# Reordering the middle stage of a two-layer hybrid encoder step: sample keys, prompt pairs, sample output, GLU

## The chip, the core and the metric

The kernel runs on one core of one Trainium2 chip. Its time is the device time of one execution in microseconds. Five engines matter here. PE (TensorE) does matrix products and transposes, with PEld loading its weights. DVE (VectorE), ACT (ScalarE) and POOL (GpSimd) do elementwise work. SP does nothing here but issue DMA transfers from its queue. Each engine works through its own list of instructions strictly in that list's order.

## The reference

The model has two layers over a prompt of 2048 tokens and a sample of 64 tokens with a cache of 2048 latents. Only the first layer is touched. In it one projection feeds two branches, latent attention and a state-space layer (S5) with a GLU:

```python
q   = (rms_norm(q_lat, g_q_lat) @ w_uq).reshape(B, T, 8, 96)        # 64 plain + 32 rotary
q_n, q_r = rms_norm(q[..., :64], ...), rope(rms_norm(q[..., 64:], ...), pos)
k_n = rms_norm(einsum('bkc,chd->bkhd', lat_all, w_uk), g_k_nope)   # lat_all = cache + new for the sample
v   = einsum('bkc,chd->bkhd', lat_all, w_uv)
o_mla = attend_chunk_causal(...)   # prompt        o_mla = attend(...)   # sample
z = gelu(s5_scan(u, ...))
z = z * sigmoid(z @ w_glu + b_glu)                                 # 512 x 512 product per token
mixed = concat([o_mla * silu(gate_mla), z * silu(gate_s5)])
return x + mixed @ w_out, ...
```

For the sample, attention multiplies the probabilities with the latents first and with w_uv afterwards.

## The kernel before

The program has four phases: a (projections, up to 540 us), b (the middle stage, up to about 921 us), c (prompt attention, up to about 1455 us) and d (output projection and the convolution layer). Products are made as three products of split numbers (`mm3`, lines L71 to L73: high by high, low by high, high by low); ACT makes the high half and DVE or POOL the low half by a subtraction. A scheduler in the compiler orders each engine's list from the order in which the program is written and from a model of durations; the buffers of a pool can be reused only when all readers of the previous pool are done.

Phase b, `phase_b`, runs so. `stage1` computes the scores of the sample queries against 17 chunks of keys (`km`, `ka`, `kb`, `sc`; the scores stay in `sT`, their running maximum in `smax`) and beside them the 16 pairs of the S5 output (`pa`, `pb`: `s5_pair`, `o_w`, `o_u`, result `s_z`). Then two generators run in turns: `phase_glu` (four column groups q of 528 tokens; for each, four loads of z and four of the gate g, a split into `g_zh` (ACT) and `g_zl` (POOL), 96 products into `pp`, a tanh, two DVE operations, and a split of the result into `g_mh` (ACT) and, in place of z, by POOL (L1224)) and `sample_av`. `sample_av` takes the maximum over keys into `mrow`, subtracts it (DVE L1115), exponentiates (ACT L1116), adds up the 17 chunks on POOL into `psum` (L1117), multiplies with the latents `lat` on PE (L1124, two accumulators), forms the reciprocal of the sum with a few small PE steps, and multiplies with w_uv (L1154). Then the weights w_uq, w_uk, w_uv are loaded and split again, and eight pairs of prompt blocks follow (`p_load`, `p_mm`, `p_norm`, `p_tr`): a pair loads `i_ql` and `i_cT`, makes queries (`pq`), keys and values (`pp`), stores the values (L664), normalizes, transposes and stores `s_kT` and `s_qT`. The rest of the GLU runs between their steps. After phase b, the buffers of the head with index 0 (`c_kx`) are opened, and phase c loads head 0 in four pieces and splits them on ACT and DVE (L1279, L1280); heads from 1 on are split on POOL (L1282, L1283), which also scales every softmax row (L1319).

## Time and profile before

| what | value |
| --- | --- |
| runs | 2441.78, 2442.80, 2450.74 us, median 2442.8 us |
| profiled execution | 2443.96 us, span 2442.1 us |
| busy share of the span | PE 92%, PEld 82%, DVE 76%, ACT 48%, POOL 58% |
| granted PE clock, mean | 0.969 of full speed |
| chain that ended last | PE 63%, DVE 8%, DMA 6%, ACT 3%, POOL 2% |
| bytes moved | 354 MB, 145 GB/s mean |

The profiled execution is about 1 us above the median of the runs; all sums below are made against its own time of 2443.96 us. PE is busy nearly all the time except in the middle stage: of 40 equal slices of the span the page gives PE 7, 6 and 8 tenths in those around 690, 750 and 930 us. The chain's shares say which engine the end waited for; a busy share in itself does not, since an idle engine off that chain costs nothing.

### The profile page before, as it was taken

What the parts mean: (1) busy time and instruction counts of PE and PEld (TensorE: products, weight loads), DVE (VectorE), ACT (ScalarE), POOL (GpSimd) and SP (SyncE); (2) the same over time, 40 slices, a digit from 0 to 9 for tenths busy, and PEclk for the clock granted to TensorE, in tenths of its full rate; (3) what the DMA queues carried; (4) which work ended last, traced back from release to release, by engine and by line L of the source; (5) the groups of instructions that cost most, each with busy time, mean ns of one, the idle gap of its engine ahead of it and who ended that gap; (6) DMA issues with size and microseconds to landing.
All of it is one profiled execution on the core that took longest, in us unless ns stands there. A gap on an engine that the chain in (4) does not pass through costs nothing.

```text
span 2442.1 us, 39230 instructions
## 1 busy us (share of the span) xinstructions
PE 2245.7 (92%) x13613; PEld 2004.2 (82%) x13613; DVE 1861.3 (76%) x3986; ACT 1181.5 (48%) x2196; POOL 1413.3 (58%) x1281
## 2 busy tenths in 40 slices
PE   6788989989986987999999999999999999989996
PEld 6788979986655876888888888988888889879996
DVE  7772346975473776888787865999999999999994
ACT  4343345236543665777777754433433533533433
POOL 5232543117382545777777444586768888876861
PEclk9999999999998997999999999999999999999998
DMA  8887575326665873222222337665355346434452
GB/s 190 198 221 166 132 177 151 87 63 186 162 161 155 257 221 85 72 69 67 69 70 70 92 126 255 235 186 177 103 172 180 95 129 212 146 127 134 147 171 89
DMA packets 347590, 354.29 MB, mean 145 GB/s; under 512 B 149760, under 2 KB 285248, under 8 KB 347392
## 3 DMA queue, kind: packets, MB, share of 16 engines
q1 hardware_dynamic: 346688, 350.60, 50.5%
q8 instruction: 108, 1.77, 0.3%
q10 hardware_dynamic: 704, 1.18, 0.2%
q14 instruction: 90, 0.74, 0.1%
HBM read 257.91 MB, written 93.52 MB: 144 GB/s over the span
## 4 chain that ended last, share of the span: by engine, by line
PE 63%; DVE 8%; DMA 6%; ACT 3%; issue 2%; POOL 2%; SPq 1%; DVEq 0%; ACTq 0%; POOLq 0%
PE pp L71 14%; PE pp L72 14%; PE pp L73 14%; PE pt L1338 4%; PE s_ps L1295 3%; PE o L1359 2%; PE o L1358 2%; PE s_ps L1296 2%; PE s_ps L1297 2%; DMA kl<-s_kT 1%; DMA s_v<-v_hl 1%; DVE acc L1648 1%; DVE sT L1115 1%; PE ps L552 1%; PE ps L550 1%
## 5 line engine op out<-in xcount | busy, mean ns | idle before, releaser
L1648 DVE SCALAR_TENSOR_TENSOR acc<-vt,cw,acc 128x384 f32<-128x384 f32 (+2 forms) x1142 | 671.2, 660 | 2.1 <-ACT acc L1634 0.5
L1844 POOL TENSOR_TENSOR wl<-wr,wh 128x1024 fp32r<-128x1024 f32 x110 | 265.3, 2413 | 119.6 <-ACT wh L1843 119.6
L1843 ACT ACTIVATE wh<-wr 128x1024 fp32r<-128x1024 f32 x136 | 144.1, 1060 | 325.7 <-PE pp L72 166.8
L1348 DVE TENSOR_TENSOR ptl<-pt,pth 128x512 fp32r<-128x512 f32 (+2 forms) x320 | 186.2, 602 | 30.2 <-ACT pth L1347 29.0
L1347 ACT ACTIVATE pth<-pt 128x512 fp32r<-128x512 f32 (+2 forms) x320 | 161.9, 528 | 92.4 <-PE pt L1338 90.6
L71 PE MATMUL pp<-b0h,wh 128*128 128x512 f32 (+1 forms) x488 | 181.3, 372 | 7.6 <-ACT b0h L1751 6.0
L73 PE MATMUL pp<-b0h,wl 128*128 128x512 f32 (+1 forms) x488 | 180.4, 370 | 0.0
L72 PE MATMUL pp<-b0l,wh 128*128 128x512 f32 (+1 forms) x488 | 180.3, 370 | 0.0
L1319 POOL TENSOR_SCALAR s_sb<-s_sb,s_st 128x1024 f32<-128x1024 f32 (+7 forms) x128 | 118.3, 937 | 103.7 <-DVE s_st L1315 65.4
L1844 POOL TENSOR_TENSOR w<-wr,w 128x1024 fp32r<-128x1024 f32 x57 | 137.4, 2410 | 61.6 <-ACT w L1843 59.2
L71 PE MATMUL pp<-xh,vh 128*128 128x256 f32 (+1 forms) x448 | 133.3, 298 | 31.8 <-ACT vh L191 12.0
L1843 ACT ACTIVATE w<-wr 128x1024 fp32r<-128x1024 f32 x64 | 67.9, 1060 | 175.2 <-PE pp L72 103.4
L1359 PE MATMUL o<-ptl,v 128*128 128x256 f32 x576 | 150.7, 299 | 0.1
L1358 PE MATMUL o<-pth,v 128*128 128x256 f32 x576 | 149.0, 285 | 0.7 <-ACT pth L1347 0.6
L1295 PE MATMUL s_ps<-kh,qh 96*128 96x512 f32 (+3 forms) x320 | 132.7, 415 | 11.4 <-DVE s_sm L1300 9.9
L73 PE MATMUL pp<-xh,vl 128*128 128x256 f32 (+1 forms) x448 | 131.5, 294 | 1.7 <-DVE mx L208 1.7
L71 PE MATMUL pp<-xh,wh 128*128 128x256 f32 (+1 forms) x384 | 115.0, 299 | 19.0 <-ACT qsum L229 10.9
L72 PE MATMUL pp<-xl,vh 128*128 128x256 f32 (+1 forms) x448 | 131.8, 294 | 0.0
L1338 PE MATMUL pt<-ident,s_sb 128*128 128x128 f32 x800 | 121.4, 277 | 11.2 <-POOL s_sb L1319 8.6
L1311 ACT ACTIVATE s_sb<-s_sb,s_st 128x1024 f32<-128x1024 f32 (+6 forms) x128 | 122.0, 956 | 8.7 <-DVE s_st L1303 8.3
L1296 PE MATMUL s_ps<-kh,ql 96*128 96x512 f32 (+3 forms) x320 | 117.1, 366 | 0.0
L1297 PE MATMUL s_ps<-kl,qh 96*128 96x512 f32 (+3 forms) x320 | 117.0, 366 | 0.0
(521 smaller groups left out, 7606.8 us busy)
## 6 DMA issues: line engine op xcount, KB each, us to landing
wr<-w_c SPq DMA_DIRECT2D x120, 512.0 KB, 3.5
wr<-w_o SPq DMA_DIRECT2D x80, 512.0 KB, 3.6
raw<-xT SPq DMA_DIRECT2D x28, 512.0 KB, 5.0
raw<-x SPq DMA_DIRECT2D x16, 512.0 KB, 5.5
s_v<-v_hl SPq DMA_DIRECT2D x8, 1024.0 KB, 7.2
tb<-s_x SPq DMA_DIRECT2D x32, 256.0 KB, 3.1
raw<-w_m SPq DMA_DIRECT2D x15, 512.0 KB, 6.9
v<-s_v SPq DMA_DIRECT2D x15, 512.0 KB, 5.1
```

What stands on the lines that cost most here:

```text
L71: mm(o, wh, xh, start=first, stop=False)
L72: mm(o, wh, xl, start=False, stop=False)
L73: return mm(o, wl, xh, start=False, stop=last)
L1295: nc.tensor.matmul(o[:, :n], t["qh"][:, q], t["kh"][:, k0:k0 + n], start=True, stop=False)
L1296: nc.tensor.matmul(o[:, :n], t["ql"][:, q], t["kh"][:, k0:k0 + n], start=False, stop=False)
L1338: nc.tensor.transpose(p[:, i, :], sb[:, (c + i) * 128:(c + i + 1) * 128], self.ident)
L1348: nc.vector.tensor_tensor(ptl[:, c:c + m, e:e + 128], p[:, :m, :], f(pth[:, c:c + m, e:e + 128]), op=OP.subtract)
L1358: nc.tensor.matmul(w, v[:, c, :], pth[:, c, lo:], start=c == 0, stop=False)
L1359: nc.tensor.matmul(w, v[:, c, :], ptl[:, c, lo:], start=False, stop=c == 2 * a + 1)
L1648: stt(box[i], vt[:, k:k + n], cw[:, ct, k:k + 1], src, op0=OP.mult, op1=OP.add)
L1843: act(h, r, AF.Copy)
L1844: (nc.vector if vec_split(slots[i]) else nc.gpsimd).tensor_tensor(l, r, f(h), op=OP.subtract)
```

## The change

Phase b is written in another order. After `stage1` the maximum is taken at once (`av_max`), then the pairs run alone, with the split w_uq and w_uk that phase a left in place (`self.bw`) instead of reloaded ones. Then the buffers of head 0 are opened, and `sample_av` and `phase_glu` follow, so the GLU runs last and alone. The sum of the exponentials is a third product per chunk, with ones as weights, into a third accumulator; POOL's additions, the zeroing of `psum` and the small products for the sum go away, and the reciprocal is taken on 128x512 numbers in place of 128x4. The latents are loaded in four pieces of 512 KB, the GLU weights in one of 1 MB, ahead of the pairs. In `stage1` two S5 pairs stand ahead of the first cache loads, and the rotary table of the sample shrinks to the rows that it needs.

```diff
@@ -137,9 +137,10 @@
...
-            x = cp.tile([128, G, 32], F32, name=tr + nm)
-            nc.sync.dma_start(x, A[tr])
-            nc.gpsimd.tensor_tensor(x, x, g[:, None, :].to_broadcast([128, G, 32]), op=OP.mult)
+            n = rows.stop - rows.start
+            x = cp.tile([128, n, 32], F32, name=tr + nm)
+            nc.sync.dma_start(x, A[tr][:, rows])
+            nc.gpsimd.tensor_tensor(x, x, g[:, None, :].to_broadcast([128, n, 32]), op=OP.mult)
@@ -427,8 +428,8 @@
...
+            pp = self.pool(es, "b_pp", 3, PSUM)
...
-            pp = self.pool(es, "b_pp", 3, PSUM)
@@ -449,9 +450,9 @@
...
-            def q_mm(sp, qp, w, m, pq, pn):
+            def q_mm(sp, qp, w, m, pq, pn, bufs=2):
...
-                raw = sp.tile([128, 2, 384], F32, name="q_raw")[:m]
+                raw = sp.tile([128, 2, 384], F32, name="q_raw", bufs=bufs)[:m]
@@ -495,7 +496,7 @@
             def stage1():
...
-                self.rope_tab(s1, "q", math.sqrt(32.0))
+                self.rope_tab(s1, "q", math.sqrt(32.0), slice(16, 17))
@@ -560,15 +561,17 @@
...
-                raw, sq = q_mm(s1, (q[:, 0], q[:, 1]), wuq, 64, pp, "pp")
+                raw, sq = q_mm(s1, (q[:, 0], q[:, 1]), wuq, 64, pp, "pp", 1)
...
+                pa(0)
+                pa(1)
...
-                pa(0)
-                q = q_norm(s1, raw, st, 16, 64)
+                pb(0)
+                q = q_norm(s1, raw, st, 0, 64, 1)
@@ -585,8 +588,8 @@
...
-                PIPE = ((lc_load, 4), (km, 3), (ka, 2), (kb, 1), (sc, 0), (pa, 1), (pb, 0))
-                seen = {lc_load: 4, km: 1, pa: 1}
+                PIPE = ((lc_load, 4), (km, 3), (ka, 2), (kb, 1), (sc, 0), (pa, 2), (pb, 1))
+                seen = {lc_load: 4, km: 1, pa: 2, pb: 1}
@@ -605,29 +608,15 @@
...
-            self.s5es.close()
-            eg = ExitStack()
-            glu = self.phase_glu(eg, pp)
-            att = self.sample_av(eav, ap, pt)
-            NA = 10
-            for i in range(16):
-                next(glu, None)
-                if i < NA:
-                    for _ in range(18 * (i + 1) // NA - 18 * i // NA):
-                        next(att, None)
-                if i == NA:
-                    for _ in att:
-                        pass
-                    eav.close()
-                    break
+            hs = self.pool(eav, "h_s", 1)
+            self.av_max(ap, pt)
+            wgr = hs.tile([128, 4, 512], F32, name="wg_r")
+            nc.sync.dma_start(wgr, A["w_glu"])
...
+                sp = self.pool(e2, "b_s", 2)
...
-                sp = self.pool(e2, "b_s", 2)
...
-                wuq = load_w(sp, wp, "w_uq", 3, 768)
-                wuk = load_w(sp, wp, "w_uk", 2, 512)
-                wuv = load_w(sp, wp, "w_uv", 2, 512)
-                self.rope_tab(wp, "q", math.sqrt(32.0))
+                wuq, wuk = self.bw["w_uq"], self.bw["w_uk"]
@@ -698,23 +687,39 @@
...
+                wuv = load_w(sp, wp, "w_uv", 2, 512)
+                self.rope_tab(wp, "q", math.sqrt(32.0))
...
-                        next(glu, None)
...
-                        next(glu, None)
...
-                for _ in glu:
-                    pass
-                eg.close()
+            self.s5es.close()
+            self.kxes = ExitStack()
+            self.kx = self.pool(self.kxes, "c_kx", 1, None, "right")
+            eg = ExitStack()
+            eacc = ExitStack()
+            glu = self.phase_glu(eg, pp, wgr)
+            att = self.sample_av(eacc, hs, pt)
+            for i in range(16):
+                for _ in range(2):
+                    next(att, None)
+                next(glu, None)
+                if i == 8:
+                    for _ in att:
+                        pass
+                    eacc.close()
+                    eav.close()
+            for _ in glu:
+                pass
+            eg.close()
@@ -1054,7 +1059,7 @@
...
-        w = sp.tile([128, 2, 2, 128], F32, name="o_w", bufs=2)
+        w = sp.tile([128, 2, 2, 128], F32, name="o_w", bufs=3)
@@ -1074,76 +1079,69 @@
...
-    def sample_av(self, es, cp, pt):
+    def av_max(self, sp, pt):
+        nc = self.nc
+        p = pt.tile([128, 512], F32, name="pt").rearrange("p (a b) -> p a b", a=4)
+        for i in range(4):
+            nc.tensor.transpose(p[:, i], self.smax[:, i * 128:i * 128 + 128], self.ident)
+        st = sp.tile([128, 4], F32, name="st")
+        nc.vector.tensor_reduce(st, p, axis=AX.X, op=OP.max)
+        self.mrow = sp.tile([128, 512], F32, name="mrow")
+        o = pt.tile([128, 512], F32, name="pt")
+        for i in range(4):
+            self.bcast(o[:, i * 128:i * 128 + 128], st[:, i:i + 1], 128)
+        nc.scalar.copy(self.mrow, o)
+
+    def sample_av(self, es, sp, pt):
...
-        sp = self.pool(es, "h_s", 2)
...
-
-        def rows(col):
-            o = pt.tile([128, 512], F32, name="pt")
-            for i in range(4):
-                self.bcast(o[:, i * 128:i * 128 + 128], col[:, i:i + 1], 128)
-            return o
-
-        p = pt.tile([128, 512], F32, name="pt").rearrange("p (a b) -> p a b", a=4)
-        for i in range(4):
-            nc.tensor.transpose(p[:, i], self.smax[:, i * 128:i * 128 + 128], self.ident)
-        st = sp.tile([128, 8], F32, name="st", bufs=1)
-        nc.vector.tensor_reduce(st[:, :4], p, axis=AX.X, op=OP.max)
-        mrow = sp.tile([128, 512], F32, name="mrow", bufs=1)
-        nc.scalar.copy(mrow, rows(st))
-        acc = [pl.tile([128, 512], F32, name=f"acc{i}") for i in range(2)]
-        psum = sp.tile([128, 512], F32, name="psum", bufs=1)
-        nc.vector.memset(psum, 0.0)
+        acc = [pl.tile([128, 512], F32, name=f"acc{i}") for i in range(3)]
...
-        XB = 3
-
-        def load(i):
-            c = order[i]
-            if c < 16:
-                lat[c] = sp.tile([128, 256], F32, name="lat", bufs=XB)
-                nc.sync.dma_start(lat[c], A["latc"][128 * c:128 * c + 128])
+        wv = sp.tile([128, 2, 512], F32, name="wv")
+        gm = sp.tile([128, 4, 64], F32, name="o_g")
+
+        def load(b):
+            t = sp.tile([128, 4, 256], F32, name="lat", bufs=2)
+            nc.sync.dma_start(t, A["latc"][512 * b:512 * b + 512].rearrange("(c p) d -> p c d", p=128))
+            for i in range(4):
+                lat[4 * b + i] = t[:, i]
...
-            tt(x, x, mrow[:m], op=OP.subtract)
+            tt(x, x, self.mrow[:m], op=OP.subtract)
...
-            nc.gpsimd.tensor_tensor(psum[:m], psum[:m], x, op=OP.add)
...
         def av(i):
...
-            x = self.sT[:64 if c == 16 else 128, c]
+            m = 64 if c == 16 else 128
+            x = self.sT[:m, c]
+            mm(acc[2], self.ones[:m].to_broadcast([m, 128]), x, start=i == 0, stop=i == 16)
+            l = self.clat_s if c == 16 else lat.pop(c)
...
-                l = self.clat_s[:, k * 128:k * 128 + 128] if c == 16 else lat[c][:, k * 128:k * 128 + 128]
-                mm(acc[k], l, x, start=i == 0, stop=i == 16)
-            lat.pop(c, None)
-
-        for i in range(XB):
-            load(i)
-        for i in range(4):
+                mm(acc[k], l[:, k * 128:k * 128 + 128], x, start=i == 0, stop=i == 16)
+
+        load(0)
+        load(1)
+        for i in range(3):
...
+        nc.sync.dma_start(wv, A["w_uv"])
+        nc.sync.dma_start(gm, S["gm"][:, :, TP:].rearrange("h p t -> p h t"))
         for i in range(17):
...
-            if i + XB < 17:
-                load(i + XB)
-            if i + 4 < 17:
-                prob(i + 4)
+            if i and i % 4 == 0 and i // 4 + 1 < 4:
+                load(i // 4 + 1)
+            if i + 3 < 17:
+                prob(i + 3)
...
-        wv = sp.tile([128, 2, 512], F32, name="wv", bufs=1)
-        nc.sync.dma_start(wv, A["w_uv"])
-        p = pt.tile([128, 512], F32, name="pt")
-        for i in range(4):
-            mm(p[:, i:i + 1], psum[:, i * 128:i * 128 + 128], self.ones, start=True, stop=True)
-        nc.vector.reciprocal(st[:, 4:8], p[:, :4])
-        r = sp.tile([128, 512], F32, name="rrow", bufs=1)
-        act(r, rows(st[:, 4:8]), AF.Copy)
-        pls = sp.tile([128, 2, 512], F32, name="pls", bufs=1)
+        r = sp.tile([128, 512], F32, name="rrow")
+        nc.vector.reciprocal(r, acc[2])
+        pls = sp.tile([128, 2, 512], F32, name="pls")
@@ -1152,18 +1150,16 @@
...
-            g = sp.tile([128, 64], F32, name="o_g")
-            nc.sync.dma_start(g, S["gm"][hp, :, TP:])
-            r_ = sp.tile([128, 64], F32, name="o_r")
-            tt(r_, o, g, op=OP.mult)
-            rh = sp.tile([128, 64], F32R, name="o_h")
-            rl = sp.tile([128, 64], F32R, name="o_l")
+            r_ = sp.tile([128, 64], F32, name="o_r", bufs=2)
+            tt(r_, o, gm[:, hp], op=OP.mult)
+            rh = sp.tile([128, 64], F32R, name="o_h", bufs=2)
+            rl = sp.tile([128, 64], F32R, name="o_l", bufs=2)
...
-    def phase_glu(self, es, pg):
+    def phase_glu(self, es, pg, wr):
@@ -1177,10 +1173,8 @@
...
-            r = cp.tile([128, 512], F32, name="wg_r", bufs=2)
-            nc.sync.dma_start(r, A["w_glu"][:, k])
-            act(wh[:, k], r, AF.Copy)
-            gt(wl[:, k], r, f(wh[:, k]), op=OP.subtract)
+            act(wh[:, k], wr[:, k], AF.Copy)
+            gt(wl[:, k], wr[:, k], f(wh[:, k]), op=OP.subtract)
@@ -1232,8 +1226,8 @@
...
+            sp = self.pool(es, "c_s", 2)
...
-            sp = self.pool(es, "c_s", 2)
@@ -1921,8 +1915,6 @@
...
-            k.kxes = ExitStack()
-            k.kx = k.pool(k.kxes, "c_kx", 1, None, "right")
```

The list of DVE after the last score of `stage1` (smax). `g_g` and `g_r` belong to the GLU, `sT`/`mrow` to the sample softmax, `w_uvl` to the weights of the pairs, `st<-k_sq`, `st<-q_sq` and `v_hl` to the first pair. Before:

```order
L1211 TENSOR_TENSOR g_g<-g_z,g_g 128x528
L1221 SCALAR_TENSOR_TENSOR g_g<-g_r,g_g 128x264
L1095 TENSOR_REDUCE st<-pt 128x4
L1221 SCALAR_TENSOR_TENSOR g_g<-g_r,g_g 128x264
L1115 TENSOR_TENSOR sT<-sT,mrow 64x512
L1115 TENSOR_TENSOR sT<-sT,mrow 128x512 x16
L1241 MEMSET mq 1x64
L1244 MEMSET mk 1x64
L1221 SCALAR_TENSOR_TENSOR g_g<-g_r,g_g 128x264 x3
```

With the change (lines have moved by two and more, so L1115 is L1117 now):

```order
L555 TENSOR_TENSOR smax<-ps,smax 128x512 x8
L1088 TENSOR_REDUCE st<-pt 128x4
L1117 TENSOR_TENSOR sT<-sT,mrow 64x512
L1117 TENSOR_TENSOR sT<-sT,mrow 128x512 x16
L605 TENSOR_TENSOR w_uvl<-q_raw,w_uvh 128x512 x2
L645 TENSOR_REDUCE st<-k_sq 128x8 x2
L466 TENSOR_REDUCE st<-q_sq 128x8
L467 TENSOR_REDUCE st<-q_sq 128x8
L650 TENSOR_TENSOR v_hl<-pp,v_hl 128x4x64 x2
```

All 17 subtractions, and the maximum before them, now stand ahead of the first reductions and splits of the pairs, with no GLU operation between.

The list of SP around the first loads of the GLU (`g_z`, `g_g`; `bg` and `wg_r` are its bias and weights, `s_z` the stores of the S5 output, `kr_r` rotary keys of the cache, `o_h`/`o_l` the sample output, `s_qT`/`s_kT` the last pair's results, `kl` keys of head 0). Before:

```order
L1177 DMA bg<-b_glu 128x4
L1181 DMA wg_r<-w_glu 128x512 x2
L1058 DMA o_w<-s_w_72 128x512
L1075 DMA s_z<-o_z 128x2x266
L510 DMA kr_r<-krcT 32x256
L1181 DMA wg_r<-w_glu 128x512 x2
L1075 DMA s_z<-o_z 128x2x266 x2
L1191 DMA g_z<-s_z 128x8x66
L1195 DMA g_g<-s_gs 128x8x66
```

With the change:

```order
L685 DMA s_kT<-k_t 64x4x256 x2
L1261 DMA kl<-s_kT 64x512
L686 DMA s_qT<-q_t 96x8x256
L1159 DMA s_mx_h<-o_h 128x64
L1160 DMA s_mx_l<-o_l 128x64
L1159 DMA s_mx_h<-o_h 128x64
L1185 DMA g_z<-s_z 128x8x66
L1189 DMA g_g<-s_gs 128x8x66
```

The GLU's first z load stood behind stores of the S5 output; it stands now behind two stores of `o_h` and one of `o_l`.

The list of POOL at the end of phase b (`q_t`, `q_n`: last pair; `g_z<-g_g,g_mh` and `g_zl`: GLU; `kh`, `qh`, `kl`: head 1; `s_sm`: softmax rows of head 0). Before:

```order
L481 TENSOR_TENSOR q_t_9728<-q_xr,cosTq 128x256
L482 TENSOR_TENSOR q_t_9729<-q_xr,sinTq 128x256
L483 TENSOR_TENSOR q_n<-q_t_9728,q_t_9729 128x8x16
L484 TENSOR_TENSOR q_n<-q_t_9728,q_t_9729 128x8x16
L1282 TENSOR_SCALAR kh<-kl 96x512 x2
L1319 TENSOR_SCALAR s_sm<-s_sm,s_st 128x128
L1283 TENSOR_TENSOR kl<-kl,kh 96x512
L1282 TENSOR_SCALAR qh<-ql 96x512 x2
L1283 TENSOR_TENSOR kl<-kl,kh 96x512
L1319 TENSOR_SCALAR s_sm<-s_sm,s_st 128x256
L1319 TENSOR_SCALAR s_sm<-s_sm,s_st 128x384
```

With the change:

```order
L1218 TENSOR_TENSOR g_z<-g_g,g_mh 128x8x66 x5
L1204 TENSOR_TENSOR g_zl<-g_z,g_zh 128x528 x4
L1218 TENSOR_TENSOR g_z<-g_g,g_mh 128x8x66 x4
L1204 TENSOR_TENSOR g_zl<-g_z,g_zh 128x528 x4
L1218 TENSOR_TENSOR g_z<-g_g,g_mh 128x8x66 x4
L1313 TENSOR_SCALAR s_sm<-s_sm,s_st 128x128
L1276 TENSOR_SCALAR kh<-kl 96x512 x2
L1313 TENSOR_SCALAR s_sm<-s_sm,s_st 128x256
L1313 TENSOR_SCALAR s_sm<-s_sm,s_st 128x384
L1277 TENSOR_TENSOR kl<-kl,kh 96x512
```

Before, the last pair's rotary work stood ahead of the first heads; now the last two column groups of the GLU do. Of head 1 the two splits of `kh` stand ahead of the second softmax row in both.

## Rows read from the trace of the kernel before

**Rows 1.** Windows: stretch, length, busy us of PE, PEld, DVE, ACT, POOL, PEclk, DMA share, GB/s
```profile
750.00:770.00 20.00, 7.62 (x30) 6.55 (x30) 3.39 (x4) 3.05 (x4) 3.56 (x3) 0.68 0.80 250
...
920.00:940.00 20.00, 8.81 (x25) 5.70 (x25) 4.99 (x20) 5.64 (x15) 10.80 (x14) 0.50 0.95 225
```

**Rows 2.** Chain that ended last, 640 to 780 us: start, us, what
```profile
674.79 17.04 DVE sT L1115 x10
```

**Rows 3.** Timeline of PE, stage1: start, us, what, idle before and its releaser
```profile
550.81 0.80 PE L71 MATMUL pp<-bw,lc_h 128*128 128x512 f32 x1 [5.68 <-ACT lc_h L517]
...
651.61 1.12 PE L550 MATMUL ps<-qrb,kr_r 32*128 32x512 f32 x2 [0.32 <-DVE smax L554]
...
655.24 1.12 PE L550 MATMUL ps<-qrb,kr_r 32*128 32x512 f32 x2 [0.32 <-DVE smax L554]
...
666.43 1.12 PE L550 MATMUL ps<-qrb,kr_r 32*128 32x512 f32 x2
...
668.40 0.37 PE L71 MATMUL pp<-g_zh,wgh 128*128 128x264 f32 x1
```

**Rows 4.** Sample softmax by line: duration ns min/median/max, first and last start us
```profile
L1115 DVE TENSOR_TENSOR sT<-sT,mrow x17: 673/1748/2045, 674.8 to 695.4; 128x512 f32<-128x512 f32 x16, 64x512 f32<-64x512 f32 x1
...
L1116 ACT ACTIVATE sT<-sT x17: 627/630/636, 676.4 to 696.6; 128x512 f32<-128x512 f32 x16, 64x512 f32<-64x512 f32 x1
```

**Rows 5.** Timeline of PE, first prompt pair
```profile
759.78 0.66 PE L71 MATMUL pq<-w_uqh,i_ql 128*128 128x384 f32 x1 [15.97 <-DMA i_ql<-s_ql]
...
764.10 0.34 PE L72 MATMUL pq<-w_uql,i_ql 128*128 128x384 f32 x1
764.27 0.34 PE L73 MATMUL pq<-w_uqh,i_ql 128*128 128x384 f32 x1
```

**Rows 6.** Value stores of the eight pairs by line, columns as in rows 4
```profile
L664 SPq DMA_DIRECT2D s_v<-v_hl x8: 359/360/1434, 789.2 to 903.6; - x8
```

**Rows 7.** Timeline of PE, sample probabilities by latents (x12 is six products)
```profile
736.10 5.42 PE L1124 MATMUL acc<-sT,lat 128*128 128x512 f32 x12 [1.70 <-DMA lat<-latc]
```

**Rows 8.** Reciprocals on DVE by line: busy us, mean ns of one
```profile
L843 DVE RECIPROCAL den<-den 128x16 f32<-128x16 f32 x1 | 0.3, 253 | 0.0
L1143 DVE RECIPROCAL st<-pt 128x4 f32<-128x4 f32 x1 | 0.2, 172 | 0.0
```

**Rows 9.** GLU operations by line, columns as in rows 4
```profile
L1210 POOL TENSOR_TENSOR g_zl<-g_z,g_zh x16: 1308/1330/1771, 643.7 to 786.9; 128x528 fp32r<-128x528 f32 x16
...
L1224 POOL TENSOR_TENSOR g_z<-g_g,g_mh x16: 1569/1738/2018, 660.9 to 819.5; 128x528 fp32r<-128x528 f32 x16
L1191 SPq DMA_DIRECT2D g_z<-s_z x12: 518/1081/1382, 638.6 to 689.6; - x12
```

**Rows 10.** Timeline of PE, two products of the GLU
```profile
664.03 0.28 PE L73 MATMUL pp<-g_zh,wgl 128*128 128x264 f32 x1
664.15 0.28 PE L71 MATMUL pp<-g_zh,wgh 128*128 128x264 f32 x1
```

**Rows 11.** DMA issues, 640 to 945 us: count, KB each, median us to landing
```profile
i_ql<-s_ql SPq DMA_DIRECT2D x8, 768.0 KB, 8.0
...
s_mx_h<-g_mh SPq DMA_DIRECT2D x4, 1056.0 KB, 4.8
s_mx_l<-g_z SPq DMA_DIRECT2D x4, 1056.0 KB, 6.7
...
g_z<-s_z SPq DMA_DIRECT2D x11, 264.0 KB, 5.0
...
kl<-s_krT SPq DMA_DIRECT2D x2, 128.0 KB, 6.7
```

**Rows 12.** Timeline of PE, start of prompt attention
```profile
929.74 0.80 PE L1295 MATMUL s_ps<-kh,qh 96*128 96x512 f32 x1 [6.03 <-DVE s_sm L1300]
...
938.62 0.76 PE L1295 MATMUL s_ps<-kh,qh 96*128 96x512 f32 x1 [3.02 <-DVE s_sm L1300]
```

**Rows 13.** Timeline of POOL, start of prompt attention
```profile
929.20 1.20 POOL L1282 TENSOR_SCALAR kh<-kl 96x512 fp32r<-96x512 f32 x2 [13.48 <-ACT s_sm L1311]
```

8 lines of the change are left out of this document (4 added, 4 removed).

## The prediction

> **What bounds the kernel now.** I read the windows first, to find where PE is not busy, then the chain of waits inside the middle stage, then the timelines of the engines that PE waits for there. Phases a, c and d keep PE busy, so a gain must come from 540 to 940 us. Two stretches stand out: at 750 to 770 us PE is busy for 7.6 us of 20 and its granted clock falls to 0.68, at 920 to 940 us for 8.8 of 20 at 0.50 [rows 1]. The first is the hand-over from sample to pairs: PE idles for 15.97 us until `i_ql` lands [rows 5], behind weights that are loaded again and buffers that come free late. The second is the start of prompt attention: waits of 6.03 and 3.02 us among others [rows 12]. Between 675 and 692 us the chain runs over DVE's subtractions [rows 2]: a median of 1.75 us each, though one alone takes 0.67 [rows 4], because POOL's additions run beside them. The change attacks all three. What follows is a walk along the new order; T is the end of the last sample score on PE, 668.4 us before [rows 3]. I call before's point 938.6 us, from which its attention runs without a further long wait [rows 12], the reference point.
>
> **Stage 1.** Up to T the GLU leaves. The last two intervals between scores take 11.2 us (655.24 to 666.43) against 3.63 us for an undisturbed one (651.61 to 655.24) [rows 3]: 11.2 - 7.3 = 3.9 us come off. Two earlier intervals that held GLU starts give some 1.5. The wait of 5.68 us for the first cache chunk [rows 3] is partly filled by two S5 pairs, but that load now stands behind a megabyte of S5 input, so I count 2 us. Sum -7.4 (bounds -3 to -11): T = 661.
>
> **From T to the first pair.** w_uq and w_uk are not loaded again. But the GLU weights, 1 MB, stand ahead of `i_ql` on SP, and may start only after T. `i_ql` takes 8.0 us from its issue [rows 11], so PE waits till about T + 9. Then comes a wait that the diff hides: the 17 subtractions stand ahead of the pairs' work on DVE, and the 17 exponentials on ACT among the first pair's copies. The maximum is ready 6.4 us after T as before (668.40 to 674.79 [rows 2, 3]). 17 subtractions at 0.67 to 0.69 are 11.7 us, 17 exponentials at 0.63 are 10.7 [rows 4], and six copies and splits for the pair stand between them on ACT (3.6 us at the same 0.6), two of which need w_uv from the queue behind `i_cT`. ACT copies the first queries out of their bank at about T + 24, and PE, with 57 products of the pair done (27 of 0.17 us by [rows 5], 30 of a third more columns, 11.5 us), goes on at T + 25 = 686. Bounds: T + 19, if w_uv lands early, and T + 29.
>
> **The pairs.** Value stores run from 789.2 to 903.6 us [rows 6], 114.4 us for seven intervals, 16.3 each with GLU products between and 14.3 if the 120 of them there (0.12 each [rows 10]) are taken out in full. Without the GLU I take 15.3: eight pairs are 122.4, less 11.5 done, less 40 transposes that fall later (0.12 each, taken as a GLU product), 106 us (99 to 113): 792.
>
> **Sample output.** The last pairs' normalization and transposes, for which PE waited in part after the last value store, are now covered by the products with the latents. Six of those take 5.42 us [rows 7], 0.90 each; there are 51 instead of 34, of which the 17 with ones are 15.3 us of new PE work. 51 x 0.90 and 32 transposes at 0.12 are 50 us: 842. Then the reciprocal on 128x512. Four columns take 0.172 us and sixteen 0.253 [rows 8], 6.75 ns a column, so 3.4 us for 512; the lower bound is an ordinary pass, 0.67 [rows 4]. The Trainium skill (VectorE: DVE Perf Modes, First, the fixed hardware budget) says the reciprocal is an iterative division with a repeat count of 8; an estimate by that page, 512 x 8 cycles at its 0.96 GHz, is 4.3 us, and the sum would be 0.9 us higher by it; no run here shows a reciprocal of that width yet. Two multiplications (0.67 each), sixteen small products, two splits and three stores on SP follow, about as much again, while eight transposes are still to be made. The GLU's first z load stands behind these stores and goes out at 848.
>
> **GLU.** PE's share is 384 x 0.12 = 46 us [rows 10], and nothing stands between. The operands don't come at that pace. For the first group, z loads alternate with gate loads at 1.08 us each [rows 9], so the fourth goes out 7 us after the first; 5.0 to land [rows 11], the split on ACT, POOL's 1.33 [rows 9], and 60 products (7.2) after the last operand: 22 us. Second group: `g_zl` has one buffer, so POOL starts after PE's last read; a start of some 1.5, four splits at 1.33, 60 products: 14.5 with what lies between. Third and fourth: POOL's list puts the previous group's four results (1.74 each) ahead of the splits, and the z buffer is reused only after the store of that result has landed, 6.7 us [rows 11], and the loads another 5.0: 18 each. Sum 72 us, end at 920. Bounds: 56, if these transfers take half as long with the queues empty; 82, with POOL at its longest (1.77 and 2.02 [rows 9]).
>
> **Start of attention.** Head 0 is loaded and split in good time, so the 6.03 and 3.02 us that came from those loads go. Next late is head 1. Its keys reuse the GLU's buffers: the load waits until the store of `g_mh` has landed (a tanh, a DVE operation and a split, some 2.5 us at the 0.63 of [rows 4] for 512 columns; 4.8 to land [rows 11]), takes one issue and 6.7 us [rows 11], and POOL stands still for it, with the second softmax row queued behind two splits of 0.6 each [rows 13]. So PE has three more short scores and then waits until 16.8 us after the GLU's end (9 to 20): 937. There it has 1.7 us more to do than before had at its reference point. 938.5 against 938.6: a shift of -0.1 us. From there both do the same work, with PE and DVE full, so the shift reaches the end.
>
> **Sum.** 2443.96 - 0.1; against the median of the runs, 2442.8, about 2443 us. The gaps that close (16 us ahead of the pairs, 9 after them, the slow subtractions) are paid for by 15.3 us of products with ones, 26 us of GLU time in which PE waits, and the first pair's late start. Taken as independent, the bounds (4, 5, 7, 3, 13, 6) make about 17 us either way.
>
> **Rivals.** *The gaps close after all, faster.* With the pairs gone from the queues in the GLU stage, transfers land faster than their medians, which were read amid 0.8 to 0.95 of DMA share [rows 1]. If stores and loads take half the medians, the first group starts 2 to 3 us earlier, each later one 3 to 4 and head 1 some 5, about 16 us in all: 2427 us. For it: all these transfers are short of partners then. Against: the GLU's loads are paced by their issue, 1.08 us each, whatever the queue holds.
>
> *The GLU alone is a chain that PE cannot fill, slower.* Before, PE filled the GLU's waits with pairs and sample products. Where PE waits for long its clock falls, to 0.50 at the start of attention [rows 1], and the first product after the wait of 15.97 us is listed with 0.66 us where later ones have 0.34 [rows 5]. In the GLU alone PE works 46 of 72 us. If two thirds of the 240 products that follow the last operand of each group run at the lower of the two levels (1.2 GHz instead of 2.4), 160 x 0.12 = 19 us are added: 2462 us. It decides once the granted clock between the sample output and attention stays under about 0.75. The Trainium skill (Perfetto Trace Analysis, Optimization Strategy) advises to interleave stretches of a kernel whose most contended engine differs, and this change takes such an interleaving apart; by that rule it loses.
>
> *The changed order does nothing for head 0.* If its early loads wait for the last pair's stores anyway, the shift grows by at most the 9 us of [rows 12], still within the forecast, of whose chance it has 0.05.
>
> **How the numbers follow.** Forecast, no change that can be told (0.5% or 12 us is about what a measurement of this kernel can tell from none): 0.51; the first rival 0.26, the second 0.23. Faster 0.26, same 0.51, slower 0.23. The range leaves a tenth on either side: 2425 to 2462.
>
> **What would show it.** In the changed kernel's profile: PE idle some 8 us after the last sample score until `i_ql`, and again until ACT's exponentials are through; value stores about 15.3 us apart; a reciprocal of some 3.4 us; a GLU stage of about 72 us with waits for `g_zh`, `g_zl` and z; then a wait of some 10 us on softmax rows behind POOL's `kh`. A GLU stage under 58 us makes the first rival right, one over 85 the second. I would be wrong from the start if the pairs ran at over 16.3 us, with the DMA queues as their limit.

## The result and the profile of the changed kernel

The changed kernel takes 2469.2 us (median of 4 runs, 2466.30 to 2473.13) against 2446.4 us for the kernel before beside it: ratio 1.0094, interval 1.0067 to 1.0122. Run again beside other kernels, it gave 1.0076 (1.0051 to 1.0102). So it is slower by about 0.9%, where no change was forecast, and its time lies above the range. The profiled execution has a span of 2468.3 us, 26.2 more than before.

Windows of the changed kernel (columns as in rows 1):

```profile
640.00:660.00 20.00, 15.29 (x40) 8.61 (x38) 2.08 (x3) 3.39 (x6) 2.62 (x2) 0.50 0.00 1
...
680.00:840.00 160.00, 155.47 (x743) 119.09 (x741) 104.71 (x242) 88.33 (x193) 57.32 (x76) 1.00 0.65 191
840.00:860.00 20.00, 16.31 (x90) 13.65 (x91) 9.01 (x17) 5.31 (x12) 5.23 (x4) 0.58 0.94 188
860.00:880.00 20.00, 15.67 (x102) 15.03 (x101) 14.90 (x14) 10.42 (x18) 12.90 (x8) 0.83 0.63 159
880.00:900.00 20.00, 11.90 (x74) 11.38 (x73) 9.73 (x9) 7.44 (x13) 12.53 (x8) 0.77 1.15 268
900.00:920.00 20.00, 11.83 (x81) 11.10 (x81) 11.23 (x12) 9.51 (x16) 10.03 (x7) 0.84 0.77 166
920.00:940.00 20.00, 15.63 (x97) 14.74 (x97) 9.41 (x21) 8.84 (x18) 8.60 (x6) 0.84 0.10 35
940.00:960.00 20.00, 12.60 (x41) 9.01 (x40) 5.25 (x23) 5.27 (x14) 12.51 (x18) 0.50 0.92 245
```

What the change aims at is reached: from 680 to 840 us PE is busy for 155.47 of 160 us at the full clock, where before had the hole of [rows 1]. The time is lost in what follows, the GLU from 844 us on, where PE is busy for 60 to 80% with a mean granted clock of 0.58 to 0.84, and in 940 to 960, at 0.50.

Timeline of PE in the changed kernel (the last two scores of the sample, first pair, the first products of the second to fourth GLU group, start of attention, two hand-overs of heads):

```profile
655.45 2.07 PE L551 MATMUL ps<-qrb,kr_r 32*128 32x512 f32 x2 [1.41 <-DVE smax L555]
660.94 2.07 PE L551 MATMUL ps<-qrb,kr_r 32*128 32x512 f32 x2 [1.41 <-DVE smax L555]
...
672.32 0.66 PE L71 MATMUL pq<-bw,i_ql 128*128 128x384 f32 x1 [1.92 <-DMA i_ql<-s_ql]
...
869.05 0.63 PE L71 MATMUL pp<-g_zh,wgh 128*128 128x264 f32 x3 [2.80 <-ACT g_zh L1203]
...
891.44 1.03 PE L71 MATMUL pp<-g_zh,wgh 128*128 128x264 f32 x3 [5.64 <-ACT g_zh L1203]
894.93 0.59 PE L72 MATMUL pp<-g_zl,wgh 128*128 128x264 f32 x1 [2.46 <-POOL g_zl L1204]
...
915.32 1.03 PE L71 MATMUL pp<-g_zh,wgh 128*128 128x264 f32 x3 [5.69 <-ACT g_zh L1203]
...
937.68 0.50 PE L1289 MATMUL s_ps<-kh,qh 96*128 96x512 f32 x1 [4.24 <-DVE s_sm L1294]
949.99 1.47 PE L1332 MATMUL pt<-ident,s_sm 128*128 128x128 f32 x5 [7.40 <-POOL s_sm L1313]
...
1015.44 1.77 PE L1332 MATMUL pt<-ident,s_sb 128*128 128x128 f32 x12 [2.55 <-POOL s_sb L1313]
...
1209.07 2.82 PE L1332 MATMUL pt<-ident,s_sb 128*128 128x128 f32 x12 [3.22 <-POOL s_sb L1313]
```

The GLU's first z load goes out at 844.64 us and PE's last GLU product ends at 933.4 (937.68 less the wait of 4.24): 88.8 us, forecast 72. A group takes PE from 869.05 to 891.44 to 915.32, some 23 us, and at the start of each it waits first for `g_zh` and then for `g_zl`.

### The profile page after: what moved, and what is told of

It reads as the page before. It is cut to its first block, busy times and chain, and to the rows that moved or that the text cites. A ratio compares the mean times of both kernels' runs of the same rounds, so it can differ in the third digit from the quotient of the medians.

```text
span 2468.3 us, 39252 instructions
## 1 busy us (share of the span) xinstructions
PE 2279.4 (92%) x13631; PEld 2028.0 (82%) x13631; DVE 1855.5 (75%) x3980; ACT 1173.8 (48%) x2190; POOL 1385.6 (56%) x1264
## 4 chain that ended last, share of the span: by engine, by line
PE 61%; DVE 7%; DMA 6%; ACT 4%; issue 2%; POOL 2%; SPq 0%; DVEq 0%; ACTq 0%; POOLq 0%
PE pp L71 13%; PE pp L72 13%; PE pp L73 13%; PE pt L1332 4%; PE s_ps L1289 3%; PE o L1353 2%; PE o L1352 2%; PE s_ps L1290 2%; PE s_ps L1291 2%; DMA s_v<-v_hl 2%; PE acc L1127 1%; PE ps L553 1%; PE ps L551 1%; DMA b1l<-s_mx_l 1%; DVE cab L1034 1%
## 5 line engine op out<-in xcount | busy, mean ns | idle before, releaser
L73 PE MATMUL pp<-b1h,wl 128*128 128x384 f32 (+1 forms) x312 | 111.8, 359 | 7.2 <-DVE wl L1838 6.8
```

The lines of the kernel that those rows point to most:

```text
L73: return mm(o, wl, xh, start=False, stop=last)
```

## The experiments

The GLU length in the table runs from the issue of the first z load to the end of the last `g_mh`, which can be read in all traces (in the changed kernel 844.64 to 938.69 us, 94 us; the 72 us forecast to PE's last product answer to about 77 on this scale). The attention length runs from the first `o_t` copy on ACT, the first finished piece of attention's output, to the last; it is 495 us before. Both lengths come from the one profiled execution of each kernel, which can lie some us off the median of its runs (8 us above it in e6, 6 below in e14): what stands behind attention took 1001 and 996 us in the two profiled executions of the changed kernel. The ratio is made from several runs of each.

| run | what | ratio to before (interval) | GLU, us | attention, us |
| --- | --- | --- | --- | --- |
| changed kernel | | 1.0094 (1.0067 to 1.0122) | 94 | 502 |
| e1_fill | spare products keep PE's clock | 1.0076 (1.0050 to 1.0102) | 90 | 504 |
| e2_pipe | splits written earlier, double buffers | 1.0103 (1.0077 to 1.0129) | 91 | 497 |
| e13_ml | z no longer overwritten by the result | 1.0031 (1.0013 to 1.0050) | 79 | 501 |
| e5_pipe_ml | both, other places of buffers | 1.0097 (1.0065 to 1.0128) | 75 | 511 |
| e9_glu | both, places as in the changed kernel | 1.0002 (0.9987 to 1.0017) | 74 | 497 |
| e3_c_order | old pool order of attention | 1.0052 (1.0033 to 1.0072) | 97 | 498 |
| e10_glu_c | e9 and e3 | 1.0027 (1.0005 to 1.0048) | 86 | 512 |
| e16_c_h1 | e10, head 1 split off POOL | 1.0031 (1.0010 to 1.0051) | 82 | 512 |
| e4_no_ones | no product with ones, the sum left out | 1.0018 (1.0001 to 1.0036) | 92 | 498 |
| e7_poolsum_c | e3, sum on POOL at once | 1.0110 (1.0076 to 1.0144) | 100 | 501 |
| e8_all | e5 and e7 | 1.0081 (1.0054 to 1.0109) | 85 | 505 |
| e11_glu_c_sum | e10, sum on POOL later | 0.9975 (0.9950 to 1.0000) | 85 | 496 |
| e14_glu_sum | e9, sum on POOL later | 1.0058 (1.0039 to 1.0077) | 79 | 506 |
| e17_c_h1_sum | e16, sum on POOL later | 0.9961 (0.9943 to 0.9978) | 82 | 499 |
| e6_keepw | before, with w_uq and w_uk kept | 1.0068 (1.0048 to 1.0089) | | 498 |
| e12_fill_s1 | spare products in stage 1 | 1.0170 (1.0132 to 1.0208) | | 503 |

### What makes the GLU long

**e1_fill.** Is it the clock?

```diff
+                    for n in range(48 if q and not m and not i else 0):
+                        nc.tensor.matmul(o, wh[:, 0, :128], old[:, 2, :C8], start=True, stop=True)
+                    old = mh
                     for k in range(4):
```

> Changed kernel with 48 spare products (wh by g_mh of the group before) put into the bank that the second, third and fourth GLU group fill first, ahead of their first real product. They change nothing in the result and keep PE working between two groups. Theory A (PE's low clock lengthens the GLU): 36 products in each of three groups go from 0.22 to 0.12 us, 11 us together, the GLU from 91 to 80 us, about 2458 us. Theory B (the chain of tanh, multiplication and split in ACT's, DVE's and POOL's lists sets the pace, and the low clock only follows from the waits): the clock rises, the GLU gets at most 2 us a group shorter, about 2464 us or more.

The clock rose, the stage hardly shortened. Windows of e1_fill:

```profile
860.00:880.00 20.00, 18.34 (x150) 18.14 (x150) 14.63 (x14) 10.42 (x18) 13.19 (x8) 1.00 0.58 165
880.00:900.00 20.00, 16.91 (x128) 15.72 (x127) 10.04 (x12) 9.59 (x16) 11.34 (x8) 1.00 1.13 261
900.00:920.00 20.00, 17.07 (x131) 16.06 (x131) 10.82 (x11) 8.09 (x14) 12.41 (x8) 1.00 0.69 166
```

At 1.00 in place of 0.77 to 0.84 the GLU is 4 us shorter, about as theory B has it; its ratio cannot be told from that of the changed kernel. The low clock follows from the waits, and raising it in this way gives little back. What the clock alone costs is not isolated: in the second group the real products follow the spare ones without a wait, though POOL had begun their first `g_zl` at 866.74 us, so there the spare ones stood in their way. Timeline of PE in e1_fill:

```profile
865.04 6.13 PE L1211 MATMUL pp<-g_mh,wgh 128*128 128x264 f32 x48 [1.66 <-ACT g_mh L1220]
871.00 0.29 PE L71 MATMUL pp<-g_zh,wgh 128*128 128x264 f32 x1
```

**e2_pipe and e13_ml.** Two chains could set the 23 us: the result of a group stands ahead of the next group's split on ACT and POOL, or z can be loaded again only when the result, which is written over it, has been stored. e2 cuts the first in the source, e13 the second.

```diff
             for m in range(4):
+                if m == 2 and q < 3:
+                    halve(q + 1)
```

> Changed kernel with g_zh and g_zl in two buffers and the split of the next GLU group written ahead of the third quarter of the present one, so that it no longer stands behind the last results on ACT and POOL. Theory B: a group takes about 15 us (four times 3.6 us for tanh, multiplication, split) in place of 23, three times 7 us off, about 2448 us. Theory A: as B, since PE is fed and keeps its clock; A and B differ only in the run before. Theory C (the z loads, which wait for the store of the group before last, set the pace): the splits only stand still at another place in the lists, about 2462 to 2469 us.

```diff
-            ml = z.rearrange("p k i c -> p k (i c)").bitcast(F32R)
+            ml = sp.tile([128, 4, 528], F32R, name="g_ml")
```

> Changed kernel with the low half of the GLU result in a tile of its own (g_ml) in place of z, and nothing else: the store-then-load chain of z is cut, the splits stay single and behind the results of the group before. If that chain alone set the 23 us of a group: as e9_glu, 2444 us, the stage 75 us long. If the order result, then split, then products on ACT, POOL and PE is the longer one: groups stay over 20 us, about 2465 us. If both ended at about the same time, as the trace of the changed kernel suggests: little gain from either alone (e2_pipe was the other half), 2460 us or more.

e2 gave nothing (as its theory C), e13 some 15 us of the GLU; its ratio, 1.0031, is some two thirds of the way to that of e9, between the first and the third of its outcomes. Timeline of SP, first in the changed kernel (the third group's stores and loads), then in e13:

```profile
893.18 0.37 SPq L1222 DMA_DIRECT2D s_mx_l<-g_z  x1
893.64 5.92 SPq L1189 DMA_DIRECT2D g_g<-s_gs  x4
899.98 0.77 SPq L1187 DMA_DIRECT2D g_z<-s_z  x1
...
908.25 1.31 SPq L1188 DMA_DIRECT2D g_z<-s_z  x1
```

```profile
882.80 5.77 SPq L1189 DMA_DIRECT2D g_g<-s_gs  x4
888.62 1.14 SPq L1187 DMA_DIRECT2D g_z<-s_z  x1
...
892.16 0.88 SPq L1188 DMA_DIRECT2D g_z<-s_z  x1
```

In the changed kernel the last group's z loads start 6.8 us after the store of `g_z` was issued and take until 909.6 to be issued, eight of them; in e13 they are all out at 893.0. And the order of the lists follows. Timeline of ACT in the changed kernel, then in e13:

```profile
910.15 1.15 ACT L1217 ACTIVATE g_mh<-g_g 128x528 fp32r<-128x528 f32 x1 [1.92 <-DVE g_g L1215]
913.66 1.17 ACT L1217 ACTIVATE g_mh<-g_g 128x528 fp32r<-128x528 f32 x1 [1.76 <-DVE g_g L1215]
914.63 2.24 ACT L1203 ACTIVATE g_zh<-g_z 128x528 fp32r<-128x528 f32 x4
```

```profile
903.74 2.23 ACT L1203 ACTIVATE g_zh<-g_z 128x528 fp32r<-128x528 f32 x4
905.87 4.36 ACT L1217 ACTIVATE g_mh<-g_g 128x528 fp32r<-128x528 f32 x4
```

In the changed kernel `g_zh` stands behind the last `g_mh`, which waits for DVE's product, which waits for tanh, which waits for PE: each quarter takes 3.5 us (910.15 to 913.66), and PE has nothing to do for 5.69 us. With z free earlier, in e13, the scheduler puts all four splits ahead of the results, without a line of the source that asks for it. In e2, where the z loads still wait for the store, the splits of the third and fourth group came out behind the results again, and nothing was gained. Timeline of ACT in e2_pipe, fourth group:

```profile
910.09 1.17 ACT L1226 ACTIVATE g_mh<-g_g 128x528 fp32r<-128x528 f32 x1 [1.76 <-DVE g_g L1224]
911.06 2.24 ACT L1199 ACTIVATE g_zh<-g_z 128x528 fp32r<-128x528 f32 x4
```

**e5_pipe_ml and e9_glu.** Both cuts at once.

```diff
+            ml = sp.tile([128, 4, 528], F32R, name="g_ml")
...
+                if m == 2 and q < 3:
+                    halve(q + 1)
...
-        r = sp.tile([128, 512], F32, name="rrow")
+        r = self.smax
...
-        pls = sp.tile([128, 2, 512], F32, name="pls")
+        pls = self.sT[:, 0:2]
```

> As e2_pipe, but the low half of the result gets a tile of its own (g_ml) in place of z, so that the z loads of a later group no longer wait for the store of an earlier one (to make room, the reciprocal and the normalized sample output are written over smax and the first two chunks of sT). Theory G (two chains of like length set the 23 us of a group: result of one group ahead of the split of the next on ACT and POOL, and store, then load, of z): with both cut, a group takes some 15 us, three groups save 24, about 2445 us. Rival H (DVE and POOL slow each other, 3.5 us for each quarter of a group whatever the order): 18 to 19 us for a group, about 2456 us. Rival A (the clock alone): no more than e1_fill, 2462 us.

The GLU came out at 75 us, as theory G has it, but the time didn't move. With 6 KB less room taken under the pairs' buffers, these lie elsewhere, the split of the GLU weights no longer has to wait for them, and POOL does it beside the first pair. Timelines of POOL and, with the 17 subtractions (10.32 us in the changed kernel), of DVE in e5_pipe_ml:

```profile
674.13 5.94 POOL L1177 TENSOR_TENSOR wgl<-wg_r,wgh 128x512 fp32r<-128x512 f32 x4 [27.38 <-ACT wgh L1176]
```

```profile
676.11 12.93 DVE L1117 TENSOR_TENSOR sT<-sT,mrow 64x512 f32<-64x512 f32 x17 [4.28 <-ACT mrow L1093]
```

The first value store came at 697.83 us in place of 689.50, and the GLU began 9 us later. It still ended 11 us earlier, and the first `o_t` copy came 8 us earlier (957.6 against 965.5); an attention 9 us longer took that back, which was not traced to a cause. In e9 an unused tile restores the places (and `mrow` serves in place of `smax`):

```diff
+                self.pool(e2, "b_0", 1).tile([128, 1536], F32, name="pad")
                 sp = self.pool(e2, "b_s", 2)
```

> As e5_pipe_ml, with 6 KB of unused room under the pairs' buffers, so that these lie where they lie in the changed kernel and the split of the GLU weights stays behind the pairs; the pairs should then start as in the changed kernel. Theory G (GLU chains): the stage from the first z load to the last result takes 75 us, as in e5_pipe_ml, in place of 94, and most of it reaches the end: 2469 - 19 = 2450 us. Rival: head 1, whose loads wait for the store of the last group, takes back some 7 us of it at the start of attention, 2457 us.

Measured 1.0002: with the GLU 20 us shorter the change costs nothing, which was the forecast. The long GLU is the main cause of the slow-down: the first `o_t` copy comes at 948.1 us, 17.4 earlier than in the changed kernel, though the wait for head 1 is still there (8.18 us). A further 5 us come from a shorter attention, which the edit wasn't made for. e13, one line of that edit, has 13 of the 17 us and almost none of the 5.

### The start of attention

**e3_c_order, e10_glu_c, e16_c_h1.**

```diff
-            sp = self.pool(es, "c_s", 2)
             kps = (self.kx, self.pool(es, "c_k", 1))
+            sp = self.pool(es, "c_s", 2)
```

> Changed kernel with the two pools of the attention phase opened in the old order (buffers of odd heads first, then the common ones). Theory E (the shift grows from 18 to 26 us inside attention because of that order): the growth goes, about 2461 us. Rival F (it grows because the heads' loads meet other moments of the POOL list after a late start): unchanged, 2469 us, with the same single waits at the hand-over of heads.

> e9_glu with the attention pools in the old order. If both are separate causes: 2469 - 19 - 12 = 2438 us, and no wait of PE of over 4 us at the start of attention. Rival (the old order only moves the wait to head 1's buffers that GLU tiles still hold): as e9_glu.

In e3 head 1 is loaded amid the GLU, PE's wait of 7.40 us at 949.99 is gone, and the kernel is some 10 us faster, though head 1's splits cost the GLU 3 us. The shift then grows by 3 us within attention (9.3 us at the first `o_t` copy, 12.1 at the last) where the changed kernel's grows by 6.7 (18.9 to 25.6): theory E holds for this growth; the 10 us at the start it did not have. In e10 the same edit gave nothing, for reasons that neither expectation had. The first is in the GLU. Timeline of POOL in e10_glu_c:

```profile
877.33 2.50 POOL L1286 TENSOR_SCALAR kh<-kl 96x512 fp32r<-96x512 f32 x2
...
892.93 2.50 POOL L1287 TENSOR_TENSOR ql<-ql,qh 96x512 fp32r<-96x512 f32 x2
895.39 5.10 POOL L1201 TENSOR_TENSOR g_zl<-g_z,g_zh 128x528 fp32r<-128x528 f32 x4
```

Head 1's splits run for 18 us ahead of the four splits that the GLU waits for, and the GLU is 12 us longer than in e9. Even so the first `o_t` copy comes at 945.6 us, 2.5 earlier than in e9: the wait of 8.18 us that e9 still has for head 1 is gone. The loss comes after it: attention takes 512 us in place of 497, and PE waits for POOL's softmax rows at four hand-overs of heads. Timeline of PE in e10_glu_c, two of them:

```profile
998.19 2.18 PE L1342 MATMUL pt<-ident,s_sb 128*128 128x128 f32 x9 [3.64 <-POOL s_sb L1323]
...
1065.28 2.82 PE L1342 MATMUL pt<-ident,s_sb 128*128 128x128 f32 x12 [3.92 <-POOL s_sb L1323]
```

e16 gives head 1's splits to ACT and DVE:

```diff
-                        spread(cum[n - 9] - LEAD, cum[n - 2] - LEAD, 8, lambda i, h=h: halves(h, "kq"[i % 2], 512 * (i // 2)))
+                        spread(cum[n - 9] - LEAD, cum[n - 2] - LEAD, 8, lambda i, h=h: halves(h, "kq"[i % 2], 512 * (i // 2), h == 1))
```

> e10_glu_c with the splits of head 1 on ACT and DVE, as head 0's, in place of POOL. In e10 POOL split head 1 between 877 and 895 us, in the middle of the GLU, and the third group came 27 us after the second in place of 15. If that is why the old pool order gave nothing there: the GLU ends at 920 as in e9_glu, PE has no wait of over 4 us at the start of attention, and the time is 8 to 10 us below e9_glu, 2435 us. Rival: the splits now stand in the GLU's way on ACT and DVE instead, 2445 us or more.

The rival's time came (2450.9 us), its reason only in part. The GLU is 4 us shorter than in e10, and the first `o_t` copy came 8 us earlier than in e9 (939.8 against 948.1). But attention takes 512 us again, with four hand-over waits of 3.94 to 4.80 us (the first, of 4.48, at 993.24), and that took back the 8 us and some 7 more. Why these waits are longer than in e9 (2.33 and 2.37 us at most) was not settled.

### The product with ones and the sum on POOL

```diff
-            mm(acc[2], self.ones[:m].to_broadcast([m, 128]), x, start=i == 0, stop=i == 16)
```

> Changed kernel without the product with ones: the sum over the exponentials is left out and the reciprocal is taken of the first accumulator in its place. If the product lies on the path as counted, 17 times 0.90 = 15 us come off, about 2454 us. Rival: the pair's late transposes or the loads of the latents set the end of that stretch, and at most 5 us come off, 2464 us or more.

The reciprocal starts at 819.20 us in place of 836.50: 17 us, where 15.3 were counted, and they reach the end (a ratio lower by 0.0076, 18.6 us). e7 adds the sum up on POOL instead:

```diff
+            nc.gpsimd.tensor_tensor(psum[:m], psum[:m], x, op=OP.add)
...
+        mm(acc[2], self.ones.to_broadcast([128, 128]), psum, start=True, stop=True)
```

> Changed kernel with two parts undone: the attention pools in the old order (as e3_c_order), and the sum over the exponentials added up by POOL, with one product with ones at the end in place of seventeen. If e4_no_ones and e3_c_order add: 2469 - 17 - 11 = 2441 us. Rival: POOL's additions, about 1.1 us each, slow the subtractions again (1.7 in place of 0.67 us each) ahead of the first pair, and give up to 17 us back, 2458 us.

Timelines of DVE (the 17 subtractions) and of PE in e7_poolsum_c:

```profile
669.81 24.47 DVE L1119 TENSOR_TENSOR sT<-sT,mrow 64x512 f32<-64x512 f32 x17 [2.79 <-ACT mrow L1093]
```

```profile
687.58 0.80 PE L71 MATMUL pp<-w_uvh,i_cT 128*128 128x512 f32 x1 [7.35 <-ACT k_sq L644]
696.01 0.80 PE L72 MATMUL pp<-w_uvl,i_cT 128*128 128x512 f32 x1 [7.64 <-DVE w_uvl L605]
```

The rival held: beside POOL's additions (1.6 us each, not 1.1) the subtractions take 24.47 us (10.32 in the changed kernel), and PE waits 15 us for what stands behind them. In e11, e14 and e17 the additions begin only with the third pair:

```diff
+                    if P == 3:
+                        nc.gpsimd.tensor_scalar(self.psum, box[2][2][0][1], 0.0, 1.0, op0=OP.mult, op1=OP.mult)
```

> e10_glu_c with the sum over the exponentials added up on POOL beside the third and later pairs (its first operation waits for a key tile of the third pair), and one product with ones at the end. If POOL has room there: 17 us less than e10_glu_c, 2421 us. Rival: POOL's additions slow DVE and with it the pairs, 5 to 10 us given back, about 2430 us.

> e9_glu with the sum over the exponentials on POOL beside the third and later pairs, the attention pools as in the changed kernel. If the gain of the sum in e11 against e10 (12 us) holds here: 2444 - 12 = 2432 us, 0.5% faster than before. Rival: what the sum gives is lost at the start of attention, where head 1's keys wait for the GLU's last store: 2440 us.

> e16 with the sum over the exponentials on POOL beside the third and later pairs (as e11). If e11's gain against e10 holds: 12 us less than e16, 2423 us, a kernel faster than both. Rival, by e14, in which the same sum gave nothing: 2435 to 2445 us.

Against their partners without it, e11 gained 0.5%, e17 0.7%, e14 lost 0.6%. Most of this is not a gain of the sum itself. The pairs pay for POOL's additions (last value store 8 to 11 us later), and the GLU's first load goes out only 1 to 6 us earlier, not 17. Up to the first `o_t` copy e11 is 1.0 us ahead of e10 and e17 0.5 ahead of e16; the rest is attention, 496 and 499 us in place of 512, in which the long waits of e10 and e16 are gone. The longest one left in e11:

```profile
1121.16 1.75 PE L1347 MATMUL pt<-ident,s_sb 128*128 128x128 f32 x12 [2.23 <-POOL s_sb L1328]
```

e14 starts its GLU 5.7 us earlier than e9 but has lost that by the GLU's end, and its attention is 9 us longer (505.8 us from the first `o_t` copy to the last, 496.7 in e9). Why attention differs so much among these kernels was not settled. e17 is the one kernel whose interval lies below 1: 2435.3 us, 0.4% below before. e8, which joins e5 and e7, had e7's cost at the start and e10's in the GLU:

> e5_pipe_ml and e7_poolsum_c together. If the three costs (products with ones, GLU chains, late head 1) are separate: 2441 - 24 = 2417 us. Rival: head 1 is no longer late once its loads don't wait for the GLU, so an earlier GLU end meets another limit there (its first rows on POOL), and half of it is lost, about 2430 us.

### Parts in the kernel before, and stage 1

```diff
-                wuq = load_w(sp, wp, "w_uq", 3, 768)
-                wuk = load_w(sp, wp, "w_uk", 2, 512)
+                wuq, wuk = self.bw["w_uq"], self.bw["w_uk"]
```

> Kernel before with one part of the change alone: the split w_uq and w_uk that phase a left are used for the pairs and not loaded and split again; the order stays (sample output and GLU in turns, then pairs with the rest of the GLU). If the 16 us wait ahead of the pairs comes from these loads and splits: 10 to 14 us faster than before, about 2432 us. Rival (the pair's buffers come free only when the sample output is done, so i_ql waits anyway): no more than 4 us, 2440 us or more.

Timeline of PE in e6_keepw:

```profile
781.44 0.69 PE L71 MATMUL pq<-bw,i_ql 128*128 128x384 f32 x1 [14.40 <-DMA i_ql<-s_ql]
```

The rival held, and worse: the wait for `i_ql` is 14.40 us (15.97 before), and the kernel is 0.7% slower. By the code the kept weights hold the room that the GLU's buffers took over, the first z load goes out at 672.77 us (638.6 before [rows 9]), and the GLU no longer fills the end of stage 1.

```diff
+                    for n in range(8 if 6 <= g < 16 else 0):
+                        mm(o, wuk[0][:, 0, :m], wuk[1][:, 0], start=True, stop=True)
```

> Changed kernel with 8 spare products ahead of each of the last ten sample scores of stage 1, into the bank that the score then fills. If the low clock of PE lengthens the end of stage 1: the last scores come 4.0 to 4.4 us apart in place of 5.5, the end of the last one 5 us earlier, 2464 us. Rival (copy, maximum and split on ACT and DVE set the pace of the scores): at the full clock the scores stay 5.5 us apart, 2469 us or, with the spare products in the way, more.

Timeline of PE in e12_fill_s1:

```profile
655.79 1.12 PE L553 MATMUL ps<-qrb,kr_r 32*128 32x512 f32 x2
659.41 3.68 PE L552 MATMUL ps<-bw 128*128 128x512 f32 x8 [1.41 <-DVE smax L557]
```

At a granted clock of 0.99 (640 to 660 us) the score and its maximum take 3.62 us (5.49 at 0.50, 655.45 to 660.94 above), so theory and rival were both half right: the clock is worth 1.9 us a score, but with a single bank for the scores the spare products stand in the way for 2 to 3.6 us.

The changed kernel once more:

> The changed kernel itself once more, beside the two others. Its time should be 2469 us within 5, and its waits at the hand-over of heads the same as in its first profile (2.55 us in the second head, 3.22 us in the fifth) if they come from the program, and others if they come from the run.

2463.65 us, span 2462.9; the same two hand-overs show waits of 2.56 and 3.13 us, and attention takes 503 us (502). What the shift gains within attention belongs to the program.

## Why the prediction was wrong

- **Stage 1.** T came at 665, not 661. The GLU's products, counted as a burden there, had also kept PE's clock up: from 640 to 660 us it is at 0.50, and five scores stand 5.49 us apart, not 3.63. Window of before, in which it is at 0.91:

```profile
640.00:660.00 20.00, 17.41 (x99) 12.93 (x98) 7.57 (x12) 9.25 (x17) 5.26 (x4) 0.91 1.08 208
```

- **First pair.** Its product begins at 672.32 us, T + 7.3 (T + 9 predicted). The second wait until T + 25 does not show. Subtractions and exponentials stand where the order says, at their undisturbed times, but w_uv had landed early, and ACT copies the first queries out at T + 19.5, near the early bound (T + 19); PE goes on with the next queries at 685.86 us, T + 20.8, without a wait. Lines of the changed kernel (ACT's copy; subtractions and value stores with columns as in rows 4):

```profile
684.49 0.48 ACT L461 COPY q_raw<-pq 128x384 f32<-128x384 f32 x1
```

```profile
L1117 DVE TENSOR_TENSOR sT<-sT,mrow x17: 673/676/684, 671.1 to 680.7; 128x512 f32<-128x512 f32 x16, 64x512 f32<-64x512 f32 x1
...
L653 SPq DMA_DIRECT2D s_v<-v_hl x8: 360/360/1029, 689.5 to 792.4; - x8
```

- **Pairs and sample output: right in the prices, by luck in the time.** These lines answer to [rows 4, 6]: value stores 14.7 us apart (15.3), the last at 792.4 (792). That the last one agrees is luck: T came 4 us late, and the wait that was counted after it wasn't there. The reciprocal took 3.35 us (3.4; the two rows continued to 512 columns give 3.6), and the first z load came at 844.64 (848), with the product with ones a little above its price (17 us by e4, 15.3 counted). For that reciprocal the prediction's estimate from the Trainium skill (VectorE: DVE Perf Modes, First, the fixed hardware budget) was 4.3 us; the trace goes with the rows.
- **GLU: the step that failed.** From one last product to the next, read back from the waits above (866.25, 885.80, 909.63, 933.44), the groups take 21.6, 19.6, 23.8 and 23.8 us; the first was right (22), the others were priced at 14.5, 18 and 18. The steps were there (four results on POOL ahead of the splits, z free only after its store), but they were priced, at 18 us without a sum, as if the split began when z arrived. In the lists it stands behind the last result, which is a chain of its own through PE, ACT, DVE and ACT again, 3.5 us a quarter; and the loads were counted at 5.0 us to land, not with 5 to 10 us to issue four to eight of them one by one. With z's load free of the store, PE's stage takes 72.4 us (846.44 to 918.85 in e13), as long as the sum, which had that store in it: they agree by chance.
- **The second rival** came nearest in time (2462), and its sign came, a GLU stage over 85 us, but by the wrong share: it priced the clock at 19 us, and raising it in e1 gave 4. The chain that PE cannot fill, its title, was right.
- **Start of attention: the wait was right, its treatment was not.** PE resumes at 949.99, 16.6 us after the GLU's end (16.8). The line of POOL that answers to [rows 13]:

```profile
948.27 1.20 POOL L1276 TENSOR_SCALAR kh<-kl 96x512 fp32r<-96x512 f32 x2 [7.49 <-DMA kl<-s_krT]
```

  But it was taken as given, where the diff held its cause: with the pools in the old order (e3) it goes. And behind it PE runs at 0.50 with POOL's splits between softmax rows, 6 us more than counted up to the first `o_t` copy (shift 18.9; 12.9 where PE resumes).
- **"The shift reaches the end"** was wrong by 7 us: PE's waits between the first and the last `o_t` copy add up to 20.7 us, 13.8 before, the longest of them at hand-overs of heads behind POOL's rows (2.55 and 3.22 us, 2.23 at most before). Why POOL is later there was not traced.

Together: the GLU ends 13.4 us late (4 from T, -7.4 up to the z load, 16.8 in the GLU). Where PE resumes the shift is 12.9, with the 6 after it 18.9, with 7.3 within and behind attention 26.2.

The Trainium skill (Perfetto Trace Analysis, Optimization Strategy) says that interleaving stretches whose most contended engine differs may help; taken as a rule, it would have given the right sign. e9, in which the stretches stay apart and the loss is gone, shows that the missing neighbour alone doesn't make it: the chain within the GLU does for the most part.

## What to carry over

A stage that is moved out of another's shadow must be priced as a chain: from the last operation of one group to the first of the next, through every in-order list on the way, with the issue of its loads. A buffer that is reused for a result can delay more than its load: with z free earlier (e13), the scheduler also put the splits at another place in ACT's list. Look in a diff for pools that change places: what lies where decides which transfer can go early, and a transfer that goes early brings its splits along. And before a gain is put down to an edit, see in the trace in which stage it arose: of e11's gain of 0.5% almost nothing arose where the edit was.
